# Moving a background's transfers to GpSimd's queue and some stores to ScalarE's queue, in a hybrid decoder block

## The chip, the cores and the metric

The kernel runs on one core of one Trainium2 chip. The metric is the time of one execution on the device in microseconds (us), given as the median of the runs. The engines are named as the profile names them: PE is the matrix engine (TensorE), DVE is VectorE, ACT is ScalarE, POOL is GpSimd, and SP is SyncE, which here only issues transfers. SPq, ACTq and POOLq are the instruction streams of those engines where they issue a transfer; each stream is in order, so a transfer that has to wait holds up everything behind it on the same engine.

## The reference: what is computed

One layer of a residual trunk over 2048 tokens of 1024 channels in float32:

```
h   = RMSNorm(x);  u = h @ W_in               (1024 -> 3584 columns)
y_A = B * conv3(C * v);  y_B = RG-LRU(conv4(x_r)) * gelu(g)
x   = x + concat[RMSNorm(y_A), RMSNorm(y_B)] @ W_out
x   = x + relu(RMSNorm(x) @ W1)^2 @ W2        (1024 -> 4096 -> 1024)
out = RMSNorm(x)
```

The change touches the two MLPs (the line with W1 and W2) and a piece of work that runs behind the first of them.

## The kernel before, in words

**Blocks and pairs.** The tokens are cut into four blocks of 512, and the MLP is computed for two blocks at a time: the *first pair* (blocks 0 and 1) and the *second pair* (blocks 2 and 3). The first pair's mixers and output projections come first, block after block; then comes its MLP, from about 473 to 1098 us of the profiled execution; then the second pair's mixers, projections and MLP.

**The MLP.** Every large product is computed by a scheme with seven products in place of eight (Strassen's, in the variant with shared sums), so weights and results are added and subtracted on DVE around the products. The first half (class `Up`) runs over eight slabs `s` of 512 hidden channels, with seven products each, in the order `ORDER = (1, 2, 6, 5, 7, 3, 4)`. A product is 24 matmuls of 128x512; float32 accuracy is reached by splitting each operand in a high part (`hi`, a cast on ACT, line 178) and a low part (`lo`, a subtraction on DVE, line 179) and multiplying three of the four combinations. So a product needs `w_hi` from ACT and `w_lo` from DVE before PE can run it. `prepare` makes them `LEAD1 = 2` products ahead in the program.

After each product `drain` takes the result out of PE's accumulators: ACT copies it (line 860, `snap`), later products are added on DVE (lines 877, 885, 889), and the finished hidden tile is put through ReLU and a square: on ACT (lines 865, 866 and 901, 902) where `self.s < 3 or self.by_act`, which in the first pair is every slab and in the second pair the first three; on DVE otherwise. Tile 2 (product 4) is squared on ACT in every slab. Seven combinations `z` of the four tiles are then stored to DRAM (`keep`, `spill`, line 776) and fetched back (`fetch`, `refill`, line 781) for the second half, class `Down`, whose products are called `dn`. Before the change every one of these transfers is issued by SP.

**The background.** The second pair computes its input and output projections by the same scheme, and for that it needs sums of the weights `w_in` and `w_out`. The generator `prepare_sums` makes them behind the first pair's work: it loads weight tiles (lines 1245 and 1258 before; tiles `w_in`, `w_out`, three buffers of the pool `xp` while `in_mlp` holds), adds and subtracts on DVE (lines 1276 to 1312), splits (ACT `sum_hi`, DVE line 179) and stores both parts to DRAM (`put`, line 1224, `d_sum`). It goes in *steps*: one step of it is issued after a product, in the first half from product 14 to the seventh from the end and not after product 3, so after six products of seven; seven steps make one *unit*, the sums of one column or row group. `step` issues under `tc.issue_after(made_at["sp"])`: the step's work stands behind the last spill or refill noted there.

**What sets the order.** PE's order in the MLP is the order of the program text (`tc.manual_schedule`). On ACT, DVE, SP and POOL in the first pair's MLP a scheduler orders the instructions at build time, from its own estimate of when each can run; on the chip each engine then runs its list strictly in order. Tiles live in pools with a fixed number of buffers, so a load waits until whoever used the buffer last is done, which can be a store's transfer.

## Time and profile before

| | us |
|---|---|
| median of 3 runs (lowest, highest) | 2133.34 (2132.09, 2136.24) |
| the profiled execution, its own time | 2131.97 |
| its span in the profile | 2129.9 |
| PE busy in the span | 2106.1 |
| DVE busy | 1611.4 |
| ACT busy | 1097.6 |
| POOL busy | 44.7 |

Read the page from the span downwards: the busy share of each engine first, then what released the idle time of the engine that is busy nearly always, then where in the span that idle time lies. A group of instructions carries its line, its engine, its tiles, the count, the mean duration and the idle time just before it with the releaser. In views by window the number behind an engine's busy time is the count of instructions, and PEclk is the clock granted to PE as a share of full speed. For a transfer the profile gives the time its issue took on the issuing engine and, apart from that, the time to landing.

### The profile page before, as it was taken

The page shows a single profiled execution, that of the slowest core. Times are in us where ns is not written, and L with a number is a line of the kernel's source. Part 1 is how long each engine was busy: PE and PEld are TensorE (multiplying, and loading weights), DVE is VectorE, ACT ScalarE, POOL GpSimd, SP SyncE. Part 2 cuts the span into 40 slices and gives each one's busy share as a digit, 9 for nine tenths or more (in the row PEclk, how much of TensorE's full clock was granted, in tenths as well). Part 3 has the DMA queues.
Part 4 walks back from the last instruction along what each step waited for, and adds up shares of the span by engine and source line. Part 5 has one row for each costly group of instructions (what it writes and reads, how often), then busy time and mean ns, then how long its engine had stood idle before and what let it go on. Part 6 is the DMA issues. An engine that isn't in the chain of part 4 may idle for free.

```text
span 2129.9 us, 25132 instructions
## 1 busy us (share of the span) xinstructions
PE 2106.1 (99%) x9396; PEld 1728.9 (81%) x9396; DVE 1611.4 (76%) x1865; ACT 1097.6 (52%) x1410; POOL 44.7 (2%) x62
## 2 busy tenths in 40 slices
PE   9999999999999999999999999999999999999998
PEld 7888888788887878888888777888788888888886
DVE  6889547858766767989997776785886666887776
ACT  6884357626554544444455888323664333333344
POOL 0000000000000000000000100000000000000000
PEclk9999999999999999999999999999999999999999
DMA  9988889643577778587755565776334354844432
GB/s 333 330 316 299 335 333 352 254 178 105 193 267 293 271 282 342 195 310 278 265 213 203 194 213 210 291 253 236 124 133 164 120 206 189 340 154 158 139 119 79
DMA packets 204875, 493.50 MB, mean 232 GB/s; under 512 B 15825, under 2 KB 80337, under 8 KB 204753
## 3 DMA queue, kind: packets, MB, share of 16 engines
q1 hardware_dynamic: 203056, 487.18, 63.2%
q10 hardware_dynamic: 1696, 4.72, 0.6%
q8 instruction: 74, 1.21, 0.2%
q14 instruction: 49, 0.39, 0.1%
HBM read 325.11 MB, written 166.72 MB: 231 GB/s over the span
## 4 chain that ended last, share of the span: by engine, by line
PE 87%; DVE 6%; ACT 3%; DMA 2%; issue 1%; SPq 0%; POOL 0%; DVEq 0%; POOLq 0%; ACTq 0%
PE up L848 40%; PE dn L966 27%; PE po L260 5%; PE ps_x L233 2%; PE wo_x L1786 2%; PE ps_g L233 2%; PE wo_w L1786 2%; PE ps_c L233 1%; PE wo_y L1786 1%; PE psri L1408 1%; DVE w_lo L179 1%; PE dn L985 1%; DVE xr L648 1%; PE start_x L509 1%; DMA raw<-in_w_out_dram 1%
## 5 line engine op out<-in xcount | busy, mean ns | idle before, releaser
L848 PE MATMUL up<-H,w_hi 128*128 128x512 f32 x2576 | 799.7, 392 | 8.8 <-ACT w_hi L178 4.4
L848 PEld LDWEIGHTS up<-H,w_hi 128*128 128x128 f32 x2576 | 483.8, 189 | 116.0 <-issue 6.7
L848 PE MATMUL up<-H,w_lo 128*128 128x512 f32 x1288 | 503.3, 391 | 1.0 <-DVE w_lo L179 1.0
L966 PE MATMUL dn<-w_lo,z_hi 128*128 128x512 f32 x864 | 336.2, 389 | 0.2 <-DVE w_lo L179 0.2
L966 PE MATMUL dn<-w_hi,z_lo 128*128 128x512 f32 x864 | 336.1, 389 | 0.0
L966 PE MATMUL dn<-w_hi,z_hi 128*128 128x512 f32 x864 | 336.1, 389 | 0.0
L848 PEld LDWEIGHTS up<-H,w_lo 128*128 128x128 f32 x1288 | 242.7, 188 | 52.3 <-DVE w_lo L179 1.9
L178 ACT CAST z_hi<-z 128x1024 fp32r<-128x1024 f32 x112 | 118.0, 1054 | 314.8 <-PE dn L966 224.4
L179 DVE TENSOR_TENSOR w_lo<-w,w_hi 128x1024 fp32r<-128x1024 f32 x156 | 190.2, 1221 | 67.8 <-PE dn L966 24.7
L178 ACT CAST w_hi<-w 128x1024 fp32r<-128x1024 f32 x156 | 163.1, 1050 | 134.4 <-PE up L848 64.0
L966 PEld LDWEIGHTS dn<-w_lo,z_hi 128*128 128x128 f32 x864 | 162.2, 188 | 34.3 <-DVE w_lo L179 0.6
L966 PEld LDWEIGHTS dn<-w_hi,z_hi 128*128 128x128 f32 x864 | 162.2, 188 | 33.8
L966 PEld LDWEIGHTS dn<-w_hi,z_lo 128*128 128x128 f32 x864 | 162.2, 188 | 33.5
L179 DVE TENSOR_TENSOR z_lo<-z,z_hi 128x1024 fp32r<-128x1024 f32 x112 | 136.5, 1219 | 24.3 <-ACT z_hi L178 24.3
L998 DVE TENSOR_TENSOR x<-dn,x 128x1024 f32<-128x1024 f32 x108 | 131.3, 1220 | 31.1 <-PE dn L966 30.4
L860 ACT COPY snap<-up 128x1024 f32<-128x1024 f32 x48 | 48.6, 1012 | 65.4 <-PE up L848 65.4
L865 ACT ACTIVATE snap<-snap 128x1024 f32<-128x1024 f32 x33 | 35.0, 1062 | 58.2 <-DVE snap L889 20.2
L179 DVE TENSOR_TENSOR w_lo<-raw,w_hi 128x1024 fp32r<-128x1024 f32 x44 | 53.2, 1218 | 11.0 <-ACT w_hi L178 8.8
L260 PE MATMUL po<-w_hi,y_lo 128*128 128x512 f32 x192 | 59.6, 392 | 0.7 <-DVE y_lo L590 0.7
L260 PE MATMUL po<-w_lo,y_hi 128*128 128x512 f32 x192 | 59.3, 390 | 0.9 <-DVE w_lo L179 0.9
L260 PE MATMUL po<-w_hi,y_hi 128*128 128x512 f32 x192 | 59.8, 392 | 0.0
L1786 PE MATMUL wo_x<-w_o,y_hi 128*128 128x512 f32 x192 | 59.8, 392 | 0.0
(406 smaller groups left out, 3278.0 us busy)
## 6 DMA issues: line engine op xcount, KB each, us to landing
z<-d_z SPq DMA_DIRECT2D x112, 512.0 KB, 5.5
w<-in_w_mlp_in_dram SPq DMA_DIRECT2D x64, 512.0 KB, 5.7
d_z<-snap SPq DMA_DIRECT2D x64, 512.0 KB, 2.9
w_hi<-d_w SPq DMA_DIRECT2D x55, 512.0 KB, 7.2
w_lo<-d_w SPq DMA_DIRECT2D x55, 512.0 KB, 6.8
d_z<-z SPq DMA_DIRECT2D x48, 512.0 KB, 3.3
w<-in_w_mlp_out_dram SPq DMA_DIRECT2D x48, 512.0 KB, 8.7
d_w<-w_hi SPq DMA_DIRECT2D x40, 512.0 KB, 5.8
```

The lines of the kernel that those rows point to most:

```text
L178: nc.scalar.copy(hi, src)
L179: return (lo_engine or V).tensor_tensor(lo, src, hi.bitcast(F32), SUB).ins
L233: nc.tensor.matmul(ps[:, j, lo:hi], ws[k // 4][:, k % 4, j * P : (j + 1) * P], hs[:, k, lo:hi], start=k == 0 and i == 0, stop=k == KD - 1 ...
L260: nc.tensor.matmul(ps[:, half, :], ys[:, j, t * P : (t + 1) * P], ws[j][:, 0, half * 512 : (half + 1) * 512], start=first and i == 0, stop ...
L509: nc.tensor.matmul(start_x[:, j], w[a][k // 4][:, k % 4, j * P : (j + 1) * P], h[c][:, k], start=k == 0 and n == 0, stop=k == KD - 1 and n ...
L648: V.scalar_tensor_tensor(xr[:, j, :], xr_in[:, j, k : k + TB], par("rnn_conv_w", 8 * k + c), xr[:, j, :], MUL, ADD,)
L848: nc.tensor.matmul(ps[:, j, :], ws[:, k, j * P : (j + 1) * P], hs(k), start=i in (1, 2, 5) and k == 0 and n == 0, stop=k == 3 and n == len ...
L860: nc.scalar.copy(t, ps)
L865: nc.scalar.activation(t, t, AF.Relu)
L966: nc.tensor.matmul(ps[t // 2][:, t % 2, :], zs[:, p, t * P : (t + 1) * P], ws[:, p, :], start=i in (1, 2, 5) and a == 0 and p == 0 and n == 0,
L998: V.tensor_add(xt[b, th, dh], ps[th], xt[b, th, dh])
L1786: nc.tensor.matmul(ps[t // 2][:, t % 2, :], ys[:, j, t * P : (t + 1) * P], ws[:, j, :], start=first and n == 1, stop=final and n == 6 * le ...
```

## The change

Two things change. First, while `in_mlp` holds something, that is from the start of the first pair's MLP on, the background's loads and its stores `d_sum` are issued by POOL (`behind()` returns `nc.gpsimd`); the background's earlier steps, in block 1's mixers, stay on SP. Second, a `z` tile that was squared on ACT is stored by ACT itself: tiles 1, 4 and 2 of every slab in the first pair, tiles 1 and 4 of the first three slabs and tile 2 of all eight in the second pair. The three-way combinations made on DVE stay on SP. `made_at["sp"]` now may be a store of ACT.

```diff
-    def spill(nm, t):
+    def spill(nm, t, queue=None):
         d = dp.tile(list(t.shape), F32, name="d_" + nm)
-        made_at["sp"] = nc.sync.dma_start(d, t).ins
+        made_at["sp"] = (queue or nc.sync).dma_start(d, t).ins
         return d
...
-            def keep(nm, t):
-                Z[self.s, nm] = spill("z", t)
+            def keep(nm, t, queue=None):
+                Z[self.s, nm] = spill("z", t, queue)
+
+            squares = nc.scalar if self.s < 3 or self.by_act else None
...
-                keep(1, self.c11)
+                keep(1, self.c11, squares)
...
-                keep(4, self.c22)
+                keep(4, self.c22, squares)
...
-                keep(2, c21)
+                keep(2, c21, nc.scalar)
...
         for t in (hi.bitcast(F32), src):
             d = dp.tile(W, F32, name="d_sum")
-            nc.sync.dma_start(d, t)
+            behind().dma_start(d, t)
             row.append(d)
         into[key] = row
+
+    def behind():
+        return nc.gpsimd if in_mlp else nc.sync
...
-                nc.sync.dma_start(t, src_col(w_in, COLS[unit[0]] + 256 * int(unit[1]))[0][k])
+                behind().dma_start(t, src_col(w_in, COLS[unit[0]] + 256 * int(unit[1]))[0][k])
...
-                nc.sync.dma_start(t, v[:, :, 512 * dh : 512 * dh + 512])
+                behind().dma_start(t, v[:, :, 512 * dh : 512 * dh + 512])
```

In the built program 96 transfers move from SP to POOL (20 loads of `w_in`, 12 of `w_out`, 64 stores `d_sum`) and 38 stores of `z` from SP to ACT. PE's order stays as it was but for one matmul. The scheduler orders ACT, DVE and SP anew around the moved transfers, and this is where the change is larger than its diff. Three places matter.

**ACT, slab 4.** `snap_5320` is the tile that product 3 of the slab completes (line 889 on DVE adds it up, lines 865 and 866 square it), `snap_5358` the one that product 7 completes; `w_hi_5376` is the weight of the slab's last product, 4, and `w_hi_5411`, `w_hi_5457` are those of slab 5's products 1 and 2. Before:

```order
L860 COPY snap_5320<-up_5219 128x1024
L178 COPY sum_hi_5326<-w_in_5213 128x1024
L860 COPY snap_5358<-up_5333 128x1024
L865 ACTIVATE snap_5358<-snap_5358 128x1024
L866 ACTIVATE snap_5358<-snap_5358 128x1024
L865 ACTIVATE snap_5320<-snap_5320 128x1024
L866 ACTIVATE snap_5320<-snap_5320 128x1024
L178 COPY w_hi_5376<-w1_5084 128x1024
L178 COPY w_hi_5411<-w1_5368 128x1024
L178 COPY w_hi_5457<-w1_5370 128x1024
```

And now, from the slab's first drained tiles on:

```order
L178 COPY w_hi_5376<-w1_5084 128x1024
L865 ACTIVATE snap_5244<-snap_5244 128x1024
L866 ACTIVATE snap_5244<-snap_5244 128x1024
L178 COPY w_hi_5411<-w1_5368 128x1024
L776 DMA d_z_5282<-snap_5244 128x1024
L178 COPY sum_hi_5289<-w_in_5043 128x1024
L860 COPY snap_5320<-up_5219 128x1024
L178 COPY sum_hi_5326<-w_in_5213 128x1024
L178 COPY w_hi_5457<-w1_5370 128x1024
L860 COPY snap_5358<-up_5333 128x1024
L178 COPY w_hi_5499<-w1_5368 128x1024
L865 ACTIVATE snap_5358<-snap_5358 128x1024
```

`w_hi_5376` and the two behind it stood after the squares of `snap_5320`; they now stand well ahead of them.

**SP, at the change from Up to Down.** `w2_first` are the first weights of the second half, `z_6147` and `z_6149` its first two operands, `d_z_6145` the store of slab 7's first squared tile. Before:

```order
L1224 DMA d_sum_6068<-sum_hi_5982 128x1024
L1224 DMA d_sum_6070<-w_in_5863 128x1024
L1245 DMA w_in_6072<-in_w_in_dram 128x4x256
L1245 DMA w_in_6074<-in_w_in_dram 128x4x256
L926 DMA w2_first_6107<-in_w_mlp_out_dram 128x2x512 x4
L776 DMA d_z_6145<-snap_6105 128x1024
L781 DMA z_6147<-d_z_4165 128x1024
L781 DMA z_6149<-d_z_4259 128x1024
```

And now:

```order
L776 DMA d_z_6029<-z2_6027 128x1024
L928 DMA w2_first_6107<-in_w_mlp_out_dram 128x2x512
L776 DMA d_z_6066<-z4_6064 128x1024
L928 DMA w2_first_6107<-in_w_mlp_out_dram 128x2x512 x3
L781 DMA z_6147<-d_z_4165 128x1024
L781 DMA z_6149<-d_z_4259 128x1024
```

Four background transfers and one store are gone from ahead of the two `z` loads.

**POOL, one unit of the background.** The rows run from a load to the next unit's loads; `sum_hi` tiles come from ACT, `w_in` tiles as sources of a store are sums that DVE made in place:

```order
L1250 DMA w_in_5213<-in_w_in_dram 128x4x256
L1226 DMA d_sum_5207<-sum_hi_5121 128x1024
L1226 DMA d_sum_5209<-s3_5119 128x1024
L1226 DMA d_sum_5284<-sum_hi_5246 128x1024
L1226 DMA d_sum_5286<-w_in_5041 128x1024
L1250 DMA w_in_5364<-in_w_in_dram 128x4x256
L1226 DMA d_sum_5322<-sum_hi_5289 128x1024
L1226 DMA d_sum_5324<-w_in_5043 128x1024
L1226 DMA d_sum_5360<-sum_hi_5326 128x1024
L1226 DMA d_sum_5362<-w_in_5213 128x1024
L1250 DMA w_in_5366<-in_w_in_dram 128x4x256
```

`w_in_5364` goes into the buffer of `w_in_5041`, `w_in_5366` into that of an earlier sum, so these loads wait on POOL until the store ahead of them has landed. The tile that ACT drains next by line 901 (now 903) and several of SP's `z` loads take buffers that a `d_sum` store of a few rows earlier has to leave first.

## The prediction

> **What bounds the kernel now.** I read the page's span and PE's row first, then PE's waits in the first pair's MLP (470 to 1100 us), then windows and timelines around the longest of them.
>
> ```profile
> span 2129.9 us, 25132 instructions
> PE 2106.1 (99%) x9396; PEld 1728.9 (81%) x9396; DVE 1611.4 (76%) x1865; ACT 1097.6 (52%) x1410; POOL 44.7 (2%) x62
> ...
> PE up L848 <- ACT w_hi L178: 4.4, 1, 4.4
> PE up L848 <- ACT snap L860: 2.7, 1, 2.7
> PE up L848 <- DVE w_lo L179: 0.7, 1, 0.7
> PE dn L966 <- DVE w_lo L179: 0.2, 1, 0.2
> ```
>
> PE is the bound: 2106.1 of 2129.9 us. No change of queues shortens its matmuls; it can only remove idle time or add some. The MLP holds four waits of PE, 8.0 us in all, and they sit at two places:
>
> ```profile
> 640.00:660.00 20.00, 20.00 (x89) 16.23 (x87) 7.65 (x7) 7.21 (x7) 0.00 (x0) 1.00 0.99 350
> 660.00:680.00 20.00, 14.85 (x52) 11.67 (x52) 16.67 (x15) 10.13 (x11) 0.00 (x0) 0.83 0.61 234
> 740.00:750.00 10.00, 10.00 (x46) 8.29 (x45) 9.97 (x10) 6.35 (x7) 0.00 (x0) 1.00 0.38 157
> 775.00:780.00 5.00, 2.42 (x11) 1.69 (x9) 3.69 (x4) 4.77 (x5) 0.00 (x0) 1.00 1.06 410
> 780.00:785.00 5.00, 4.92 (x15) 3.88 (x16) 5.00 (x5) 2.15 (x4) 0.00 (x0) 0.66 0.53 215
> ```
>
> The second number with an x is PE's count. Undisturbed, 20 us hold 89 matmuls, 0.225 us each. From 660 to 680 there are 52, so 37 are missing: 37 x 0.225 = 8.3 us lost, more than the waits of 4.4 and 0.7, since the granted clock was 0.83 there. From 775 to 785 there are 26, where 10 us at 0.225 hold 44.5 (46 from 740 on, with the ones at the window's edges): 18.5 are missing, 4.2 us lost, with the clock at 0.66 behind the wait. Both places together cost 12.5 us, and that is the most the change can win in this MLP.
>
> **Why PE waits there.** First place, ACT and DVE:
>
> ```profile
> 660.04 1.23 DVE L889 TENSOR_TENSOR snap<-up,snap 128x1024 f32<-128x1024 f32 x1 [4.16 <-PE up L848]
> 664.62 2.35 DVE L179 TENSOR_TENSOR w_lo<-w,w_hi 128x1024 fp32r<-128x1024 f32 x2
> ...
> 661.30 1.06 ACT L865 ACTIVATE snap<-snap 128x1024 f32<-128x1024 f32 x1 [3.23 <-DVE snap L889]
> 662.39 1.06 ACT L866 ACTIVATE snap<-snap 128x1024 f32<-128x1024 f32 x1
> 663.35 2.92 ACT L178 CAST w_hi<-w 128x1024 fp32r<-128x1024 f32 x3
> ```
>
> PE ended slab 4's product 3 at 660.0. Only then could DVE's line 889 run, then ACT's two squares, and only behind these stood the three `w_hi` casts, the first of them the weight of the very next product. That is a fault of order: ACT was idle 3.23 us with that cast behind a wait.
>
> Second place, SP and ACT:
>
> ```profile
> 758.67 2.50 SPq L1245 DMA_DIRECT2D w_in<-in_w_in_dram  x2
> 761.27 2.41 SPq L926 DMA_DIRECT2D w_first<-in_w_mlp_out_dram  x4
> 764.58 0.34 SPq L776 DMA_DIRECT2D d_z<-snap  x1
> 764.96 1.68 SPq L781 DMA_DIRECT2D z<-d_z  x2
> ...
> 763.49 1.06 ACT L866 ACTIVATE snap<-snap 128x1024 f32<-128x1024 f32 x1
> 775.23 1.05 ACT L178 CAST z_hi<-z 128x1024 fp32r<-128x1024 f32 x1 [7.63 <-DMA z<-d_z]
> 779.03 1.00 ACT L860 COPY snap<-up 128x1024 f32<-128x1024 f32 x1
> ```
>
> SP issued the `z` loads at 764.96, behind two background loads, four weight loads and a store that waited for ACT's square to end at 764.55. The first `z` landed at 775.2, ACT had waited 7.63 us for it, and the `snap` copy that frees PE's accumulator stood behind the `z` work and ran at 779.03; PE went on at 780.08.
>
> **The change, part by part.**
>
> *The new order on ACT (place 1).* `w_hi_5376` now stands ahead of the squares of product 2's tile and `w_hi_5411` right behind them, three to four products earlier in PE's terms. No wait for product 3 stands ahead of them any more. Gain 8.3 us, if the rest of ACT's and DVE's order runs in time.
>
> *SP's queue (place 2).* Gone from ahead of the `z` loads are two `w_in` loads (2.50 us of issue), two `d_sum` stores and the store that waited for the square. Without the loads SP reaches the first weight load at about 758.7 in place of 761.3, and without the store the loads follow directly: some 3 us earlier by these rows alone. PE waited 2.65 us; the wait goes or nearly goes. Gain up to 4.2 us.
>
> *38 stores on ACT.* The price of an issue there is in the trace: ACT's own `d_y` stores, and SP's issues of the same `d_z` stores above it:
>
> ```profile
> L1378 ACTq DMA_DIRECT2D d_y<-s x8: 326/336/364, 1177.8 to 1347.7; - x8
> L776 SPq DMA_DIRECT2D d_z<-snap x31: 319/339/886, 489.1 to 795.7; - x31
> 500.00:1050.00 550.00, 541.99 (x2367) 446.99 (x2367) 438.93 (x382) 270.42 (x272) 0.67 (x1) 0.99 0.72 262
> ```
>
> 24 x 0.336 = 8.1 us in the first pair's MLP (21.3 us if each took the longest, 0.886), on an engine that is busy for 270 of these 550 us; the other 14 lie in the second pair. Behind each issue stand casts, mostly for a product after the next. I take 0 on the path; without that cover it would be 0.3 us for each cast that PE waits for.
>
> *96 transfers on POOL.* No row shows a transfer issued by POOL, so its price is bounded by SP's rows for the same transfers and by POOL's own small copies:
>
> ```profile
> L1245 SPq DMA_DIRECT2D w_in<-in_w_in_dram x20: 368/832/1318, 566.6 to 841.2; - x20
> DMA to landing us min/median/max: 2.9/5.7/10.2
> ...
> L1224 SPq DMA_DIRECT2D d_sum<-sum_hi x32: 319/424/1584, 583.4 to 1014.3; - x32
> DMA to landing us min/median/max: 2.6/4.5/10.4
> ...
> 313.67 4.44 POOL L718 COPY state<-v 128x2 f32<-128x2 f32 x1 [3.59 <-DVE v L715]
> 400.02 1.05 POOL L741 COPY haloc<-cv 128x4 f32<-128x4 f32 x1 [13.62 <-DVE cv L740]
> ```
>
> An issue: between 0.32 and 4.44 us; I take 1.05, the usual copy. A landing: between 2.6 and 10.4; I take the medians, 5.7 for a load and 4.5 for a store, as the transfers share the same 72% busy DMA. POOL has nothing else to do in this MLP (0.67 us busy). Whether its transfers reach PE depends on the loop in POOL's list: load, sum on DVE (1.22), cast on ACT (1.05), subtraction on DVE (1.22), store, next load into the freed buffer, sum. With 1.05 for each issue that is (1.05 + 5.7) + 3.5 + (1.05 + 4.5) + (1.05 + 5.7) + 1.22 = 23.8 us. A unit has seven steps, six steps in seven products of 24 x 0.225 = 5.4 us: 44 us. So the background keeps pace on average. It is not only the average that counts: sums and casts of the background stand in fixed places among the weights' casts, and drains and `z` loads take buffers that a `d_sum` store leaves. Weights are prepared two products ahead, 10.8 us, which is the cover. Before, DVE did wait for such loads and PE lost nothing by it:
>
> ```profile
> DVE s L1276 <- DMA w_in<-in_w_in_dram: 15.1, 1, 15.1
> DVE w_in L1287 <- DMA w_in<-in_w_in_dram: 6.5, 2, 3.3
> ```
>
> The drains have less cover than the weights. For this I charge one new wait of the second place's size, 4.2 us (between 0 and the 32 us worked out below).
>
> The Trainium skill, "DMA: Bandwidth & Descriptors", section "Anatomy of one DMA — SWDGE (gpsimd) path", fits such a transfer by 2.0 us + bytes/436e3; for 512 KB that would be an estimate of 3.2 us, less than SP's loaded medians here, and by it alone the new wait would be 0 and the sum 2120.8. No run here shows it.
>
> *Sum.* The profiled execution took 2131.97, its span is 2129.9, and the median of the runs is 2133.34, so I work from the median: 2133.3 - 8.3 - 4.2 + 4.2 = 2125.0 us, 0.4% less. The second pair's MLP only loses stores from SP; I take 0 there.
>
> **The rivals.**
>
> *S, slower: POOL's transfers come late and the shared buffers carry it to PE.* If each of the three transfers in the loop takes the longest landing of the rows above, they grow by 4.5 + 5.9 + 4.5 = 14.9 us a unit, 10.8 are covered, 4.1 are not. There are eight units, by these rows:
>
> ```profile
> L1276 DVE TENSOR_TENSOR s<-w_in x5: 1217/1219/1225, 575.0 to 833.1; 128x1024 f32<-128x1024 f32 x5
> ...
> L1301 DVE TENSOR_TENSOR t<-w_out 128x1024 f32<-128x1024 f32 x3 | 3.7, 1219 | 0.1
> ```
>
> 8 x 4.1 = 32.8 us, against the 12.5 won: 2133.3 + 32.8 - 12.5 = 2153.6. It decides from about 3.6 us more per transfer (10.8 / 3). With 3 us more still on each, 8 x 13.1 = 105 us and 2226. For it: the buffers are taken again a few rows after the store, and each wait of PE cost 1.6 times its length here (8.3 for 5.1) through the clock. Against it: POOL is free, and a queue of its own doesn't stand behind SP's weight loads.
>
> *T, DVE's work holds up POOL's transfers*, a form of S. Every DVE group that I find from 500 to 1050 is a tensor_tensor of some 1.22 us, and DVE is busy 439 of 550 us. If a transfer waited for one of them, 3 x 1.22 = 3.7 us a unit would be covered, and the time stays 2125; if for five in a row, 18.3 - 10.8 = 7.5 a unit, 60 us in all, and 2181. The Trainium skill has this trap ("SBUF — State Buffer", section "SBUF: two separate sides") for DVE operations in a two-port mode, which it says tensor_tensor hasn't; so by it only the first of the two is left, and no run here shows either.
>
> *N, no difference.* Place 1 goes, place 2 stays because the DMA engines are full there (share 1.06 from 775 to 780), and one more wait as long as place 1 comes: 2133.3 - 8.3 + 8.3 = 2133.3.
>
> **How the numbers follow.** My forecast gets 0.47, S 0.38, T in its costly form 0.05, N 0.10. About 0.2% (4.3 us) is what a measurement can tell here. Faster 0.47, same 0.10, slower 0.43. The forecast's own range is 2120 (both waits gone, nothing new) to 2129. The range for 8 in 10 starts at 2119 and has to reach into S: up to 2170 it holds the forecast, N and nearly two thirds of S and T, 0.84; I leave out S with transfers longer than any seen.
>
> **What would show it.** Right: no wait of PE on `w_hi` near 660 and none on `snap` near 780, ACT's first `z_hi` wait well under 7.63 us, POOL's landings at or under 5.7 and 4.5. Wrong: PE waiting for casts or `snap` copies released by `d_sum` or `w_in` transfers, several in each slab; POOL issues of 2 us and more; a granted clock under 1.00 in many windows between 550 and 1050. If place 1 shows a wait again, the reading of the order was wrong.

## The result and the profile after

The changed kernel takes 2136.13 us in the median against 2133.45 for the kernel before, a ratio of 1.0014 with a 95% interval of 1.0007 to 1.0020: 2.7 us slower, where 2125.0 was forecast. The page of the changed kernel, the two rows that answer to those at the start of the prediction:

```profile
span 2136.0 us, 25241 instructions
...
PE 2105.5 (99%) x9396; PEld 1727.0 (81%) x9396; DVE 1611.9 (75%) x1865; ACT 1096.4 (51%) x1410; POOL 102.4 (5%) x158
```

PE is busy 0.6 us less in a span that is 6.1 us longer, so the difference is idle time of PE. Its waits in the first pair's MLP, by line, with the total, the count and the longest in us:

```profile
PE up L848 <- DVE snap L887: 6.7, 3, 2.7
PE dn L968 <- DVE w_lo L179: 3.4, 2, 2.4
PE up L848 <- ACT snap L860: 2.1, 1, 2.1
PE dn L987 <- DVE x L1042: 0.8, 1, 0.8
```

The wait on `w_hi` is gone, the one on `snap` is still there, and there are six new ones: five in the first two rows, on drains and weights, and a small one in the last. (Line 887 is line 885 of before, one of `drain`'s additions; the lines after it are two to five higher than before.) The same by windows: start and end, length, then busy time and count of PE, PEld, DVE, ACT and POOL, the granted clock, the DMA share and GB/s:

```profile
620.00:640.00 20.00, 18.01 (x80) 14.61 (x79) 15.54 (x14) 10.96 (x11) 2.58 (x4) 1.00 0.51 187
660.00:680.00 20.00, 20.00 (x90) 16.57 (x89) 16.69 (x16) 11.38 (x12) 1.54 (x2) 1.00 0.79 290
700.00:720.00 20.00, 17.34 (x77) 14.03 (x76) 16.72 (x15) 11.14 (x11) 3.81 (x6) 1.00 0.91 327
740.00:760.00 20.00, 17.97 (x80) 14.55 (x79) 17.85 (x16) 13.14 (x13) 4.43 (x7) 1.00 0.77 278
760.00:780.00 20.00, 18.83 (x84) 15.25 (x82) 4.73 (x5) 7.03 (x8) 0.00 (x0) 1.00 1.00 366
780.00:800.00 20.00, 19.04 (x84) 15.76 (x85) 19.90 (x18) 11.63 (x12) 0.00 (x0) 1.00 0.42 170
920.00:940.00 20.00, 17.61 (x70) 14.04 (x70) 19.96 (x19) 11.00 (x12) 1.84 (x3) 0.91 0.49 180
980.00:1000.00 20.00, 18.97 (x84) 15.40 (x83) 17.17 (x16) 7.42 (x8) 2.17 (x4) 1.00 0.89 314
```

And place 2 in the kernel before, whose place 1 the prediction shows:

```profile
760.00:780.00 20.00, 17.42 (x77) 14.08 (x75) 4.91 (x5) 7.90 (x8) 0.00 (x0) 1.00 1.03 376
780.00:800.00 20.00, 19.92 (x81) 16.30 (x82) 19.80 (x18) 9.84 (x11) 0.00 (x0) 0.91 0.50 184
```

Against 90 in an undisturbed window, place 1 (660 to 680) has lost nothing, where before 38 matmuls were missing. Place 2 (760 to 800) lacks 12, before 22. The five new places lack 10, 13, 10, 20 and 6, together 59. With 0.2267 us for a matmul (three take 0.68 us in undisturbed rows of the timeline), 8.6 us came from place 1, 2.3 from place 2, and 13.4 were lost again: 2.5 us more than before. The sixth wait, at 1097.8 us, costs 5 matmuls more (350 from 1020 to 1100 us, before 355), 1.1 us.

The medians differ by 2.7 us, the two profiled executions by 5.8 (2131.97 and 2137.79). The 2.2 us that the places don't explain lie ahead of the MLP: 2105 matmuls in the first 470 us, before 2115, and 8 of the 10 are missing in the first 20 us, where no transfer has moved and where the granted clock is 0.91 in one execution and 1.00 in the other.

**What the five new waits are.** Each ends a chain in which DVE waits for a load of the background and a row that PE needs stands behind it in DVE's list. In three the profile names the load; in the other two (DVE idle 7.99 us ahead of a sum on line 1292 at 734.15, and 2.33 us ahead of line 1317 at 985.73) it names no releaser, but DVE's row starts 10.4 and 6.6 us after POOL issued such a load, and by the view of the load's line these two landed after 10.3 and 6.5 us. The sixth wait, on line 1042, stands where no background is left; its cause was not traced. The one with the largest loss, around 920 us, from the timeline of the changed kernel (start, duration, engine, line, count, and in brackets the idle time before it with its releaser):

```profile
905.18 0.72 POOL L1263 DMA_DIRECT2D w_out<-in_w_out_dram  x1 [5.63 <-DMA d_sum<-w_out]
905.90 0.57 POOL L1226 DMA_DIRECT2D d_sum<-w_out  x1
...
906.99 0.53 POOL L1226 DMA_DIRECT2D d_sum<-w_out  x1
913.02 0.72 POOL L1263 DMA_DIRECT2D w_out<-in_w_out_dram  x1 [5.50 <-DMA d_sum<-w_out]
...
919.39 1.23 DVE L1306 TENSOR_TENSOR t<-w_out 128x1024 f32<-128x1024 f32 x1 [8.71 <-DMA w_out<-in_w_out_dram]
...
925.34 0.50 PE L968 MATMUL dn<-w_lo,z_hi 128*128 128x512 f32 x1 [2.39 <-DVE w_lo L179]
```

POOL issued a `d_sum` store at 905.9, and the next load had to wait 5.5 us for such a store to land before it could take the buffer. It was issued at 913.0 and landed at 919.4. DVE stood 8.7 us in front of the sum that needs it, and the `w_lo` for PE's next product came four rows later. At 626 us it is the same chain, with POOL waiting 6.24 us for a landed store.

At 705 and 746 us the load is the fourth of its unit. With three buffers it goes into that of the tile that DVE's line 1285 reads last (at 625.56 us POOL waited 4.87 us for that line ahead of such a load):

```profile
678.73 1.23 DVE L1285 TENSOR_TENSOR w_in<-w_in 128x1024 f32<-128x1024 f32 x1
...
680.10 0.57 POOL L1226 DMA_DIRECT2D d_sum<-sum_hi  x1 [15.06 <-ACT sum_hi L178]
681.39 0.56 POOL L1226 DMA_DIRECT2D d_sum<-s  x1 [0.72 <-DVE s L179]
682.12 0.77 POOL L1250 DMA_DIRECT2D w_in<-in_w_in_dram  x1 [0.17 <-issue]
...
692.71 1.23 DVE L1292 TENSOR_TENSOR w_in<-w_in 128x1024 f32<-128x1024 f32 x1 [8.22 <-DMA w_in<-in_w_in_dram]
...
704.20 1.22 DVE L887 TENSOR_TENSOR snap<-up,snap 128x1024 f32<-128x1024 f32 x1
```

POOL had waited 15.06 us for `sum_hi` before the two stores ahead of the load could go, but that is not what held the load: its buffer came free only when line 1285 ended, at 679.96, and the stores cost it 2.2 us beyond that. It then took 10.5 us to land (the one behind the wait at 746 us, 10.3). DVE lost 8.22 us over it, then ran ten rows without a pause before it came to the drain on line 887, which frees the accumulator for PE. The load behind the wait at 988 us had itself waited 5.06 us for a sum on DVE (line 1310), and that sum 2.12 us for the load before it.

**What POOL's transfers cost.** Issues (ns: shortest, median, longest) and landings in the changed kernel, by line from 560 to 1020 us: first the stores `d_sum`, then the loads of `w_in`:

```profile
L1226 POOL DMA_DIRECT2D d_sum<-sum_hi x32: 532/534/567, 578.4 to 1000.0; - x32
...
DMA to landing us min/median/max: 2.9/6.0/9.3
```

```profile
L1250 POOL DMA_DIRECT2D w_in<-in_w_in_dram x17: 760/768/777, 579.0 to 837.1; - x17
...
DMA to landing us min/median/max: 3.9/6.8/10.5
```

An issue is cheap (0.53 and 0.77 us). A load of `w_in` lands after 6.8 us in the median, from SP before after 6.3 (shortest 3.9, longest 10.2), one of `w_out` after 6.3 (before 6.5). A store lands after 6.0 us, before after 4.5; but from SP with the ACT stores alone (below) it takes 5.5, so the queue is not shown to be the reason. In the median the transfers themselves are not what was lost; only at 705 and 746 us are slow landings a part of it. What POOL waits for ahead of its loads is the larger sum, in its groups (busy time, mean ns, idle time with releasers):

```profile
L1250 POOL DMA_DIRECT2D w_in<-in_w_in_dram x17 | 13.1, 768 | 51.0 <-DMA d_sum<-w_in 43.8 <-DVE w_in L1285 6.8 <-issue 0.2
L1263 POOL DMA_DIRECT2D w_out<-in_w_out_dram x12 | 8.7, 726 | 54.8 <-DMA d_sum<-w_out 25.8 <-DMA d_sum<-w_in 17.9 <-DVE w_out L1310 11.2
```

**Place 2.** ACT and SP at the change from Up to Down:

```profile
776.11 1.05 ACT L178 CAST z_hi<-z 128x1024 fp32r<-128x1024 f32 x1 [7.10 <-DMA z<-d_z]
...
779.90 1.00 ACT L860 COPY snap<-up 128x1024 f32<-128x1024 f32 x1
...
766.45 0.86 SPq L781 DMA_DIRECT2D z<-d_z  x2
```

Little has moved: the `z` loads are issued at 766.45 (before 764.96), while ACT's copy of the product ahead of them, which goes by PE, ran 1.4 us later as well (767.99, before 766.58); ACT waits 7.10 us for the first (7.63), and the copy that PE needs still stands behind four casts.

### The profile page after: what moved, and what is told of

Read it like the earlier page. It is cut to its first block, busy times and chain, and to the rows that moved or that the text cites. A ratio compares the mean times of both kernels' runs of the same rounds, so it can differ in the third digit from the quotient of the medians.

```text
span 2136.0 us, 25241 instructions
## 1 busy us (share of the span) xinstructions
PE 2105.5 (99%) x9396; PEld 1727.0 (81%) x9396; DVE 1611.9 (75%) x1865; ACT 1096.4 (51%) x1410; POOL 102.4 (5%) x158
## 4 chain that ended last, share of the span: by engine, by line
PE 54%; DVE 4%; DMA 3%; issue 2%; ACT 1%; POOL 0%; DVEq 0%; POOLq 0%; ACTq 0%
PE up L848 26%; PE dn L968 22%; PE wo_x L1791 2%; PE wo_w L1791 2%; DMA d_sum<-w_out 1%; PE wo_y L1791 1%; PE psri L1413 1%; DVE w_lo L179 1%; DMA w_first<-in_w_mlp_out_dram 0%; DMA w_out<-in_w_out_dram 0%; DVE z_lo L179 0%; DVE x L1000 0%; DMA d_z<-z 0%; DVE H L179 0%; PE dn L987 0%
## 5 line engine op out<-in xcount | busy, mean ns | idle before, releaser
L848 PE MATMUL up<-H,w_hi 128*128 128x512 f32 x2576 | 796.4, 390 | 10.5 <-DVE snap L887 6.7
L178 ACT CAST w_hi<-w 128x1024 fp32r<-128x1024 f32 x156 | 163.7, 1050 | 169.8 <-PE up L848 92.2
L1000 DVE TENSOR_TENSOR x<-dn,x 128x1024 f32<-128x1024 f32 x108 | 131.5, 1218 | 17.5 <-PE dn L968 14.5
```

Of the source, the lines that this page charges most:

```text
L178: nc.scalar.copy(hi, src)
L848: nc.tensor.matmul(ps[:, j, :], ws[:, k, j * P : (j + 1) * P], hs(k), start=i in (1, 2, 5) and k == 0 and n == 0, stop=k == 3 and n == len ...
L1000: V.tensor_add(xt[b, th, dh], ps[th], xt[b, th, dh])
```

## The experiments

The theory after the first comparison: on POOL's one list the loads stand behind stores that wait for casts, and behind the landing of stores whose buffers they take; DVE then waits in front of rows that PE needs. The rivals: transfers issued by POOL are late in themselves; the ACT stores cost something; the new order on ACT and DVE would cost this on any queue. PE's count between 600 and 1020 us is one row of the windows view of one execution per kernel and measures the loss in most of the MLP by itself; the highest count of all runs is 1851, and each matmul less is 0.2267 us.

| kernel | PE's count, 600 to 1020 us | time, us | ratio to before (95%) |
|---|---|---|---|
| before | 1794 | 2133.45 | |
| whole change | 1785 | 2136.13 | 1.0014 (1.0007 to 1.0020) |
| ACT stores alone | 1822 | 2127.45 | 0.9976 (0.9965 to 0.9986) |
| POOL transfers alone | 1793 | 2133.28 | 1.0000 (0.9991 to 1.0009) |
| whole, only loads on POOL | 1801 | 2131.84 | 0.9996 (0.9987 to 1.0005) |
| whole, only stores on POOL | 1819 | 2127.85 | 0.9977 (0.9968 to 0.9987) |

### The parts of the change

ACT stores alone:

```diff
-        return nc.gpsimd if in_mlp else nc.sync
+        return nc.sync
```

> Only the 38 z stores move to ACT; the 96 background transfers stay on SP. Theory (in GpSimd's one list the background's loads stand behind stores that wait for casts and sums, a load then waits until a store has landed, DVE waits for the load in front of its list, and PE's drains stand behind it): none of the five waits of PE on drains or weights behind a background load is left. Here the weight cast w_hi_5376 stands ahead of product 3's squares, but still behind product 7's, so the wait near 660 us shrinks from the 8.3 us that PE lost to some 2 to 4; 2127 to 2133 us, ratio 0.997 to 1.000. Rival (the ACT stores cost what the whole change lost, since casts queue behind them): slower than before by the 2.7 us of the whole change or more, 2136 us and up.

Measured 2127.45 us. The ACT stores cost nothing, and by themselves win 6.0 us: place 1 lost 10 matmuls in place of 38, place 2 kept 20 missing. None of the five new waits is there. The rival falls.

POOL transfers alone:

```diff
-        made_at["sp"] = (queue or nc.sync).dma_start(d, t).ins
+        made_at["sp"] = nc.sync.dma_start(d, t).ins
```

> Only the 96 background transfers move to GpSimd; the z stores stay on SP. Theory (one list of loads and stores on GpSimd): several waits of PE behind a background load are there as in the whole change, the wait on w_hi near 660 us is gone, and the time is that of the whole change, 2134 to 2139 us, ratio 1.000 to 1.003. Rival (the ACT stores carry the loss): faster than before by up to the two old places' 12.5 us, 2121 to 2128 us, ratio 0.995 to 0.998.

Measured 2133.28 us, a little under the span given: place 1 is gone here too, and waits behind background loads are there (24 matmuls missing from 620 to 640 us, 9 from 740 to 760, 11 from 920 to 940). Both parts win place 1, which can only be won once, so their effects don't add up: -6.0 and -0.1 alone, +2.7 together. The sixth wait is there too (1.0 us), with the ACT stores alone it is not.

Only the loads on POOL, and only the stores:

```diff
 (loads alone)
-            behind().dma_start(d, t)
+            nc.sync.dma_start(d, t)
 (stores alone; both loads)
-                behind().dma_start(t, ...
+                nc.sync.dma_start(t, ...
```

> As the whole change, but of the background only the 32 loads are issued by GpSimd; the 64 d_sum stores stay on SP. Theory (loads held up behind stores in one list): a load now has a list of its own and waits for its buffer alone, so DVE's waits for w_in and w_out shrink from the 8 us and more of the whole change, PE loses little behind them, and the kernel is faster than both: 2124 to 2130 us, ratio 0.995 to 0.998. Rival (transfers issued by GpSimd are themselves late, whatever the order): the loads are what DVE waits for, so most of the 13 us lost in the whole change stays: 2132 to 2136 us.

> As the whole change, but of the background only the 64 d_sum stores are issued by GpSimd; the 32 loads stay on SP. Theory (loads held up behind stores in one list): loads no longer stand behind a store that waits for a cast, the wait near 660 us stays away since w_hi_5376 stands ahead of both squares: 2124 to 2130 us, ratio 0.995 to 0.998. Rival (transfers issued by GpSimd land late): a load still waits until a late store has left its buffer, so half of the 13 us or more stays: 2130 to 2136 us.

The stores alone on POOL behave as the theory says: 2127.85 us, as fast as with them on SP, so POOL's stores (6.1 us to landing in the median) cost nothing that the time shows. The loads alone do not: 2131.84 us, above the theory's span and at the edge of the rival's. From the timeline of that kernel:

```profile
655.20 0.75 POOL L1250 DMA_DIRECT2D w_in<-in_w_in_dram  x1 [28.82 <-issue]
...
664.66 1.23 DVE L819 TENSOR_TENSOR s<-w,w 128x1024 f32<-128x1024 f32 x1 [4.92 <-DMA w<-in_w_mlp_in_dram]
668.47 1.23 DVE L820 TENSOR_TENSOR w<-w,w 128x1024 f32<-128x1024 f32 x1 [2.58 <-DMA w<-in_w_mlp_in_dram]
```

Three loads of the background go out on POOL at 655.2, 657.7 and 659.8 us and land 6.5, 6.3 and 6.4 us later, while loads of the next slab's weights, issued by SP up to 653.5 us, land after 10.1 to 14.9 us, the last at 668.4. DVE waits 4.92 and 2.58 us for these weights, and 29 matmuls are missing from 680 to 700 us. So loads of the second list did land ahead of urgent ones issued earlier on the first. That this alone is what PE lost is not shown, since DVE's order is another as well: with the ACT stores alone the same two sums run at 663.94 and 666.22 us, hardly earlier, but the drain on line 891 stands ahead of them, at 660.54; here it stands behind them, at 669.61.

The run shows besides what holds the background's loads. Here no store stands ahead of them in their list, and they wait all the same: those of `w_in` five times for DVE's line 1285, which frees a buffer, and seven times for a landed store. So the theory as I had it (loads held up behind stores in one list) is not the cause, or not the whole of it; the buffers are the next suspect.

### The ring of three buffers

A fourth buffer for the background's tiles, with one less for the weights, where the room comes from; its control; and the partner with the background on SP:

```diff
 (four buffers, 14 weight buffers: whole change, and ACT stores alone)
-    xp = ctx.enter_context(tc.tile_pool(name="xp", bufs=3))
+    xp = ctx.enter_context(tc.tile_pool(name="xp", bufs=4))
-WSLOTS = 15
+WSLOTS = 14
 (the control: whole change, three buffers)
-WSLOTS = 15
+WSLOTS = 14
```

> The whole change with four buffers for the background's w_in and w_out tiles in place of three; the room comes from the weights' pool, 14 buffers in place of 15. Theory (the loads on GpSimd wait until a d_sum store of a few rows earlier has landed, since only three buffers go round): GpSimd's 43.8 and 43.7 us of waits for landed d_sum stores shrink to less than half, most of the five waits of PE behind a background load go, and the time falls by 5 to 10 us against the whole change: 2126 to 2131 us, ratio 0.996 to 0.999. Rival (loads stand behind stores that wait for a cast on ACT, buffers or not): the waits near 700 and 740 us stay, the time falls by under 4 us: 2132 to 2137 us.

> The control for the run before it: the whole change with the weights' pool at 14 buffers in place of 15, and three background buffers as in the change. If the fourth buffer is what helps, this one stays at the whole change's time or is slower: 2135 to 2141 us, ratio 1.001 to 1.004. If it is as fast as the run with four buffers, the new order or the smaller weights' pool made the difference, and the buffer did not.

> Only the z stores on ACT, all of the background on SP, with four background buffers and 14 weight buffers: the partner of the run of the whole change with the same buffers, whose MLP lost 6 matmuls while the missing weight buffer cost it 11 us outside the MLP. If GpSimd's queue is worth something once the ring of buffers is wide enough, this one loses more in the MLP than that one, 20 to 40 matmuls as with three buffers (30): 2137 to 2143 us, ratio 1.002 to 1.005. If the fourth buffer alone does it on any queue, it loses under 12 and takes the same time: 2132 to 2136 us.

Measured 2134.13, 2149.57 and 2142.49 us; the first time lies in the rival's span and the second above the span given. The missing weight buffer costs much more than I had thought, and outside the MLP: from 150 to 450 us PE's count falls from 1346 in the whole change to between 1281 and 1291 in these three. So I compare them with each other, by the windows view from 600 to 1020 us, in the order whole change with four buffers, its control with three, ACT stores alone with four:

```profile
600.00:1020.00 420.00, 419.57 (x1851) 347.29 (x1850) 349.64 (x304) 210.52 (x210) 53.79 (x90) 1.00 0.81 294
```

```profile
600.00:1020.00 420.00, 410.32 (x1787) 336.91 (x1786) 333.15 (x291) 204.09 (x204) 54.76 (x91) 0.99 0.79 288
```

```profile
600.00:1020.00 420.00, 414.64 (x1816) 342.40 (x1815) 339.99 (x297) 207.10 (x207) 1.07 (x1) 0.99 0.76 280
```

With the fourth buffer the whole change loses next to nothing in the MLP: 64 matmuls more than its control, 14.5 us, where the times differ by 15.4. The five waits are gone, the two near 705 and 746 us among them (PE waits 0.4 us in this MLP), against the rival that a store waiting for a cast was their cause. With the background on SP the same four buffers leave 35 missing, and the time is 8.4 us longer; but these lie at the two old places (77, 86 and 68 matmuls from 660, 680 and 780 us on, where four buffers with the whole change have 90, 90 and 87), so it is the order there that differs, and no advantage of POOL's list is shown. One link was other than expected: POOL still waits for landed stores, but next to nobody waits for POOL. The source view of the load's line, first with four buffers, then in the whole change (what POOL waited for, and who waited for the load, in us and times):

```profile
  DMA d_sum<-w_in: 50.8, 10
...
  DVE s L1281: 2.3, 1
```

```profile
  DMA d_sum<-w_in: 43.8, 11
...
  DVE w_in L1292: 14.5, 4
  DVE w_in L1285: 3.2, 1
```

The buffer doesn't shorten the wait; it lets the load be issued further ahead of need: POOL's loads of `w_out` run from 835.6 to 969.2 us, with three buffers in the control from 861.4 to 993.3.

Could the buffer be had without the price? One tile of each unit from the weights' pool while the MLP runs, with the whole change, with the stores alone on POOL, with the ACT stores alone, and with nothing else:

```diff
-        def tile_of(nm, W):
+        def tile_of(nm, W, fourth=False):
+            if fourth and in_mlp:
+                return wtile(nm, W)
```

> The whole change, with a fourth buffer for the background without taking one from the weights for good: of each unit the load that is subtracted last (a12 of w_in, b21 of w_out) takes a buffer of the weights' pool while the MLP runs, the other three go round in the three buffers as before. Theory (the whole change gives its gain back through the ring of three buffers: a load waits on GpSimd for a landed store, DVE waits for the load, drains and weights stand behind it): of the 75 matmuls lost in the whole change's MLP under 20 stay, as with four buffers (6), and nothing is lost outside: 12 us and more below the whole change, 2120 to 2126 us, ratio 0.994 to 0.997. Rival (it was the new order that came with 14 weight buffers, not the ring): 2132 to 2138 us.

> The z stores on ACT, the d_sum stores on GpSimd, the loads on SP, and the fourth buffer from the weights' pool. If GpSimd's queue for the loads is worth something once the ring is wide enough, this one is slower than the whole change with a fourth buffer by 1 us or more; if only the ring counted, both are the same within 1.5 us: 2120 to 2126 us, ratio 0.994 to 0.997.

> Only the z stores on ACT, all of the background on SP, and the fourth buffer taken from the weights' pool. If the ring matters only on GpSimd's list, this stays at the time of the ACT stores alone: 2126 to 2130 us, ratio 0.996 to 0.998. If a fourth buffer helps on any queue, it comes down to the same time as the whole change with it, 2120 to 2124 us.

> The kernel before, with nothing but the fourth buffer from the weights' pool. Theory: before the change the loads stood in SP's list and were late by that, not by the ring (SP waited 10.9 us in all for landed d_sum stores ahead of loads, GpSimd 87.5 us), so a fourth buffer doesn't remove either of the two old places: 2131 to 2138 us, ratio 0.999 to 1.002. Rival (the ring was the limit before as well): 2122 to 2129 us.

Measured 2134.17, 2130.63, 2130.24 and 2142.75 us, and against the same kernels without it that is -2.0, +2.8, +2.8 and +9.3. None of the four lies in its theory's span (the third by 0.24 us), and the first lies in its rival's. Why the kernel before loses so much by it (1754 matmuls in place of 1794) was not traced. In the first, DVE's waits for the background's loads did fall (between 500 and 1050 us from 36.5 us, the 8.0 without a named releaser among them, to 10.2), but in its profiled execution (2138.01 us, 3.8 above the median) 70 matmuls are missing all the same: PE now waits 4.6 us on `w_hi` and ACT up to 14.87 us on a weights buffer that a `d_sum` store has yet to leave. Where the fourth buffer is taken from the weights, the ring's wait moves to the weights. So this run does not repeat the gain of the four buffers.

### Place 2

First the transfer: the two `z` loads one product earlier, ahead of the eight `w_first` loads, with the ACT stores alone and with the stores on POOL:

```diff
-                    if i == 2:
+                    if i == 1:
                         downs[0].fetch(1, 0, Z)
                         downs[0].fetch(1, 1, Z)
```

> Only the z stores on ACT, and the first two z loads of the second half are issued one product earlier, ahead of the eight w_first loads instead of behind the first four. Theory (place 2 is a transfer that shares full DMA engines with 4 MB of w_first, so what is issued first lands first, whatever the queue): ACT's wait of 7.84 us for the first z goes, PE's wait on snap near 770 us goes with its 20 lost matmuls, 4.5 us: 2121 to 2125 us, ratio 0.994 to 0.996. Rival (the z loads wait for something else, such as a buffer): no change against the run with only the ACT stores, 2126 to 2129 us.

> The z stores on ACT, the d_sum stores on GpSimd, the background's loads on SP, and the first two z loads ahead of w_first. Theory: place 1 is gone by the order, place 2 by the earlier z loads, and the loads stand in no list behind a store; of the 38 matmuls lost in the run without the earlier z loads some 20 come back, 4 to 5 us: 2121 to 2125 us, ratio 0.994 to 0.997. Rival (place 2 is not set by the order of the transfers): 2126 to 2130 us, as without it.

Measured 2127.76 and 2128.88 us: no gain, the rival's case. ACT in the first of them:

```profile
766.75 1.05 ACT L178 CAST z_hi<-z 128x1024 fp32r<-128x1024 f32 x1 [3.66 <-DMA z<-d_z]
...
773.65 1.04 ACT L178 CAST w_hi<-w_first 128x1024 fp32r<-128x1024 f32 x1 [3.94 <-DMA w_first<-in_w_mlp_out_dram]
774.60 1.00 ACT L860 COPY snap<-up 128x1024 f32<-128x1024 f32 x1
```

The wait for `z` fell from 7.84 to 3.66 us and came back as 3.94 for `w_first`, which the `z` loads had overtaken. The DMA engines are full there (share 1.01 from 760 to 780 us in this run), and the copy stands behind all four casts.

So the order on ACT instead: the casts of the second half's first product behind the copy of product 5, with the ACT stores alone; the same with four buffers and 15 weight buffers (the memory comes from small statistics tiles and from scratch that this kernel's POOL doesn't use); and the same with the stores on POOL:

```diff
                 self.c22 = snap(self.w)
+                made_at["c22"] = made_at["snap"]
...
-                downs[0].prepare(1, i - 3)
+                with tc.issue_after(made_at["c22"]):
+                    downs[0].prepare(1, i - 3)
 (the second run besides)
-    xp = ctx.enter_context(tc.tile_pool(name="xp", bufs=3))
+    xp = ctx.enter_context(tc.tile_pool(name="xp", bufs=4))
-    sp = ctx.enter_context(tc.tile_pool(name="sp", bufs=4))
+    sp = ctx.enter_context(tc.tile_pool(name="sp", bufs=2))
-    nc = _bacc.Bacc("TRN2", ..., dynamic_dma_scratch_size=2048)
+    nc = _bacc.Bacc("TRN2", ..., dynamic_dma_scratch_size=256)
```

> Only the z stores on ACT; in addition ACT's four casts for the second half's first product stand behind the snap copy of slab 7's product 5, where they stood ahead of it. Theory (place 2 is a fault of order on ACT: the copy that frees PE's accumulator waits behind casts whose z and w_first transfers land late, in whatever order those are issued): PE's wait on snap near 765 us, 20 matmuls, goes: 4 us less than the ACT stores alone, 2122 to 2125 us, ratio 0.994 to 0.9965. Rival (PE then waits as long for the casts themselves): 2126 to 2129 us.

> As the run before it, with four background buffers and all 15 weight buffers; the room comes from the small statistics tiles (two buffers for four) and from scratch space of GpSimd's own transfers, of which this kernel has none. Theory (on SP's list the ring is not the limit): within 1.5 us of the run before it, 2121 to 2126 us. Rival (the ring costs on any list): the 10 matmuls lost near 660 us go as well, 2119 to 2122 us, ratio 0.9935 to 0.995.

> The z stores on ACT, the d_sum stores on GpSimd, the loads on SP, and the snap copy ahead of the second half's first casts. Of the 38 matmuls lost with the same queues and without that order, 24 stood at place 2 (760 to 800 us); they go, some 14 stay: 5 us less, 2122 to 2125 us, ratio 0.994 to 0.9965, the same as with the ACT stores alone and that order. Rival (GpSimd's stores bring a wait of their own there): 2126 to 2130 us.

Measured 2123.56, 2125.24 and 2122.72 us. In the first, ACT's rows:

```profile
767.74 1.01 ACT L860 COPY snap<-up 128x1024 f32<-128x1024 f32 x1 [4.42 <-PE up L848]
771.11 1.05 ACT L178 CAST z_hi<-z 128x1024 fp32r<-128x1024 f32 x1 [2.36 <-DMA z<-d_z]
```

The copy runs as soon as PE has the product, ACT still waits for `z`, and PE has no wait there at all. Place 2 was a fault of order on ACT, as place 1 was. The fourth buffer on SP's list gives no time: 1.7 us more than without it, 0.2 more than the theory's 1.5. The count between 600 and 1020 is 8 higher (1844 and 1836), but 7 of these stand from 660 to 680 us, where PE waits the same 2.0 us in both and only the granted clock differs (1.00 and 0.91). Where the 1.7 us go is not shown; the smaller statistics tiles are the suspect.

### What is left of place 1

With the ACT stores alone, `w_hi_5376` stands ahead of product 3's squares but behind product 7's. Those squares are put behind it:

```diff
                 V.tensor_add(self.c22, self.x, self.c22)
-                square(self.c22)
+                with tc.issue_after(hi_at[0]):
+                    square(self.c22)
```

Here `hi_at[0]` is the last cast that `split_into` made, which is the weight of the product after next.

> The z stores on ACT, the snap copy ahead of the second half's first casts, and in addition ACT's squares behind product 7 stand behind the cast of the weight for the product after next, so w_hi_5376 stands ahead of both squares in slab 4. Theory (place 1 is a fault of order on ACT and all that is left of it is that cast): the last 10 to 18 matmuls lost near 660 us go, and the MLP loses under 6: 2119 to 2122 us, ratio 0.9935 to 0.9955. Rival (PE waits next for what that order delays, the squares and their stores): 2123 to 2127 us.

Measured 2120.90 us, ratio 0.9949 (0.9936 to 0.9961), the fastest of all. PE's waits in its first pair's MLP, in full, and its window:

```profile
PE up L850 <- ACT snap L862: 0.9, 1, 0.9
```

```profile
600.00:1020.00 420.00, 419.14 (x1850) 346.74 (x1849) 342.61 (x299) 204.87 (x206) 0.72 (x1) 1.00 0.79 291
```

It needs none of the transfers on POOL: the stores on ACT and a few casts and squares in another order. Whether it needs the ACT stores was not tested; no run has these two orders with all stores on SP.

## Why the prediction was wrong, point by point

- **PE is the bound, and 12.5 us are to be won in this MLP: right.** The best run took 11.0 us off the kernel before beside it (2120.90 against 2131.92) and has one wait of 0.9 us left there.
- **Place 1 (8.3 us): right,** in place, cause and size (8.6).
- **Place 2 (4.2 us): wrong.** The step "some 3 us earlier by these rows alone" did not come: a `z` store took SP until 762.05 and a landed store 1.7 us more, so the loads left 1.5 us later than before, and against PE, which was 1.4 us later there, at the same point. And earlier would not have helped: with the loads issued earlier `w_first` was late in their stead. The row that decided was the position of line 860 behind four casts, which I had quoted but read as a matter of SP's queue. 2.3 us of 4.2 were won, and most of that by luck: PE's wait shrank only from 2.7 to 2.1 us, while the granted clock from 780 to 800 us, 0.91 before, stayed at 1.00.
- **ACT stores at 0: right.** They take 0.326 us each in the median, and alone they make the kernel 0.24% faster; the second pair's part shows nothing (4461 and 4463 matmuls from 1100 to 2100 us).
- **POOL's prices: the issue was under my 1.05 (0.53 to 0.77), a load's landing somewhat over what I took (6.3 to 6.8 for 5.7), a store's 6.0 for 4.5.** The 5.7 was a misreading: that view was by tile and held 14 stores of `w_in` beside the 20 loads, which alone took 6.3. The Trainium skill's fit ("DMA: Bandwidth & Descriptors", section "Anatomy of one DMA — SWDGE (gpsimd) path") gives an estimate of 3.2 us for such a transfer; the shortest store here took 2.9 and the shortest load 3.9, but the medians are about twice the fit, with DMA shares of 0.5 to 1.04 around them.
- **"One new wait of the second place's size, 4.2 us": this term failed.** There are five, and they cost 13.4 us; a sixth costs 1.1. The mean pace was right (the background's last store goes out at 1001.5 us, before at 1016.8), and I named the drains as having less cover than the weights, but I priced the wait against the weights' cover of 10.8 us and as a single one. The loop of 23.8 us was set against the 44 us of a whole unit, as if 20 us were spare; but each load waits for one of three buffers, until a store has landed or a sum on DVE is done, and the sum that needs it stands close behind in DVE's list (the load of 682.12 us went out 2.4 us before DVE had come to that sum). And the drains on line 887 stand one to ten rows behind a background sum in DVE's list, so a load that is late reaches PE within three products. With 13.4 in place of 4.2 and 2.3 in place of 4.2 the sum is 2133.3 - 8.3 - 2.3 + 13.4 = 2136.1; that it meets the measured time to a tenth is chance, since it leaves out the sixth wait.
- **Rival S had the mechanism, but the wrong threshold and price.** It was to decide from 3.6 us more for each transfer and to cost 32.8 us. The transfers are at most 1.5 us longer in the median, and the shared buffers still carried the wait to PE, through what a load waits for before it is issued. The ring of three buffers was in the text as an order of rows; its wait, 87.5 us on POOL in all, was not priced.
- **Rival N came nearest:** place 1 gone, place 2 there, and new waits somewhat longer than place 1; its 2133.3 is 2.8 under the measured time.
- **Rival T: nothing for it.** In the median loads land within 0.5 us of before while DVE is as busy as before, and the slow load of 682.12 us was under way while DVE stood idle for 8.22 us.

What stays open: each kernel has its own order on ACT and DVE, since the scheduler orders anew around every edit, so the fourth buffer's 64 matmuls hold what it gives as a buffer and what the order it leads to gives. The order was not held fixed in any run, and the fourth buffer taken from the weights did not repeat the gain. The whole change with four background buffers and all 15 weight buffers was not run; 2136.13 - 66 x 0.2267 = 2121.2 is only an estimate for it from the counts (1851 and 1785).

## What to carry to other kernels

Before pricing a transfer on another queue, ask what it waits for before it is issued (the buffer, the store that must land first, the row ahead in the new list, the engine that frees the buffer); that wait, more than the landing, is what cost time here. A background that shares an in-order engine with urgent rows needs its loads issued a step ahead, so count its buffers first. And where PE waits on a short copy or cast, look at what stands ahead of it in that engine's list: both old places went with the order of a few ACT rows, without a faster transfer.

## What the runs showed of the hardware that I had not expected

- An issue on POOL is short and steady: 0.532 to 0.567 us for 32 stores, 0.760 to 0.777 for 17 loads, where SP's issues of the same stores ran from 0.319 to 1.584 us.
- Two queues did not keep the order of issue: with the loads alone on POOL, three loads issued there from 655.2 to 659.8 us landed by 666.2, ahead of a weight load that SP had issued at 653.5 and that landed at 668.4.
- With the DMA share at 1.01, moving two of ten loads to the front left ACT's waiting for the group as it was (7.84 us of waiting became 3.66 and 3.94).
- Short waits cost PE less than the 1.6 times of before: the first five new ones, 10.1 us, took 59 matmuls, 13.4 us or 1.3 times; in four of the five windows the granted clock stayed at 1.00, and only the one around 925 us fell to 0.91.
